# Second mixer's small products as column halves: state outputs, chunk scores, and the order of the states

## The chip, the cores and the metric

The kernel runs on one core of one Trainium2 chip. The metric is the device time of one execution in microseconds; the times below are medians of several runs. The engines are called as in the profile: PE is TensorE (PEld its weight loads), DVE is VectorE, ACT is ScalarE, POOL is GpSimd, SP is the queue that issues most of the DMAs.

## The reference

A two-layer decoder trunk on one sequence of 256 tokens, width 1024, in float32. Layer 0 uses a windowed attention mixer, layer 1 a gated linear attention (GLA) in chunks of 64 tokens with 4 heads (keys of 128, values of 256); each mixer is followed by a gated feed-forward part of width 2816 with a short convolution. The change lies in the GLA mixer:

```python
q_t = q * jnp.exp(bcum)
k_t = k * jnp.exp(-bcum)
k_d = k * jnp.exp(blast - bcum)
A = jnp.where(causal, jnp.einsum('bhncd,bhnsd->bhncs', q_t, k_t), 0.0)   # scores of a chunk, 64 x 64
o_intra = jnp.einsum('bhncs,bhnse->bhnce', A, v)
kv = jnp.einsum('bhncd,bhnce->bhnde', k_d, v)                           # what a chunk adds to the state
...
state = dec[..., None] * state + inc                                    # scan over the 4 chunks
o = o_intra + jnp.einsum('bhncd,bhnde->bhnce', q_t, s_prev)             # the state's share of the output
```

Behind it follow a norm over each head, a gate `silu(r)` and the output projection.

## The kernel before

Activations stand transposed in SBUF: partitions are features, columns the 256 tokens. Large products are split into high and low float32r parts, three matmuls for one (`mm3`, lines 216 to 218); a weight tile of 128x2048 is loaded by SP (`split`, line 185), its high part made by ACT (line 191) and its low part by DVE (line 195), out of rings of four raw and three split buffers. The small products of the GLA mixer are plain float32; each of them is two LDWEIGHTS and two MATMUL instructions in the profile.

The GLA mixer treats its four heads in two pairs. For each pair:

- `masked` (lines 1113 to 1131) transposes `k_d` (line 1121, bank `kdt`) and makes the scores (line 1124, bank `a`). Two chunks are done at once: a tile of 128 tokens holds two chunks, the product is 128x128, and only its two diagonal blocks of 64x64 are wanted. ACT copies the transposed keys (line 1128), and DVE copies the scores under the mask `causal` (line 1130, COPY_PREDICATED) into `a_t`, which POOL has set to zero.
- `states` (lines 1133 to 1154) makes what chunks 0, 1 and 2 add to the state (line 1140). Chunk n lies in partitions 0 to 63 (n even) or 64 to 127 (n odd) of its tile, so the contraction uses one half of the rows of the array. ACT copies the first state (line 1146), DVE does the scan (line 1152).
- `outputs` (lines 1156 to 1181) makes the output: first scores by values (line 1164), then, accumulated in the same bank, state by queries for chunks 1 to 3 (line 1170): 128 stationary columns, 64 moving columns, 12 products for a pair of heads.
- `normed_outputs` sums squares (line 1194 on PE, from `osq`, line 1190 on DVE) and scales.

The order on PE is fixed by hand here: `in_turn` puts each group of products behind the one before. Between the groups stand the halves of the gate's large product (`gate`, bank `pr`) and of the last heads' queries and keys (`keyed`, bank `pqk`). The order is: scores of heads 0 and 1 within `keyed(2)`, their states, scores of heads 2 and 3 within `gate(0)`, outputs of heads 0 and 1, states of heads 2 and 3, and within `gate(1)` the norm of the first pair and the outputs of the second. `behind(i)` only orders an instruction after another for the planner; within one group, and for the other engines, the planner (the tile framework, which lays instructions out by a modelled timeline) chooses the order. Within the first call of `masked` it places the scores of the first head ahead of the transposes of the second.

In the first mixer, `outputs` (lines 577 and 581, bank `po`) has products with 64 stationary columns, whose results go by turns to partitions 0 to 63 and 64 to 127; `scores` (line 524, bank `s`) has 64 by 64 blocks.

Of the kernel before, what the change touches and what calls it, by code (L numbers as in the profile page):

```python
# [14 lines left out]
U32 = mybir.dt.uint32  # L15
# [3 lines left out]
P = 128  # L19
D = 1024  # L20
T = 256
# [7 lines left out]
CH = 64  # L29
# [28 lines left out]
def trunk(ctx: ExitStack, tc: tile.TileContext, I, out):  # L58
    nc = tc.nc
# [16 lines left out]
    mm = nc.tensor.matmul  # L76
# [28 lines left out]
    ident = const.tile([P, P], F32, name="ident")  # L105
# [13 lines left out]
    @contextmanager  # L119
    def behind(*those):  # L120

        with ExitStack() as st:
            for i in those:
                st.enter_context(tc.issue_after(i.ins))
            yield

    def keep_warm(n, ps=None):

        ps = bank("warm", "p") if ps is None else ps
        for i in range(n):  # L130
            i = mm(ps[:, :P], ones_d, ones_d, start=True, stop=True)
        return i
# [80 lines left out]
    def mm3(ps, a, b, start, stop):  # L213


        mm(ps, a[0], b[0], start=start, stop=False)  # L216
        mm(ps, a[0], b[1], start=False, stop=False)  # L217
        return mm(ps, a[1], b[0], start=False, stop=stop)  # L218
# [6 lines left out]
    def rstd_of(squares, n=D, tag=None, between=None):  # L225
        ps = bank("ms", tag)
        a = None
        for i, sq in enumerate(squares):
            if i and between:
                with behind(a):  # L230
                    a = between()
            with behind(*((a,) if between and a else ())):
                a = mm(ps[:, :T], ones_d, sq, start=(i == 0), stop=(i == len(squares) - 1))
        ln = tmp.tile([P, T], F32, tag="ln", name="ln", bufs=2)
        nc.scalar.activation(ln, ps[:, :T], AF.Ln, bias=eps[:, 0:1], scale=D / n)
        r = tmp.tile([P, T], F32, tag="rstd", name="rstd", bufs=2)
        norm_ops[:] = a, nc.scalar.activation(r, ln, AF.Exp, scale=-0.5)
        return r
# [117 lines left out]
    def parts(w, at, n=P):  # L356
        return w[0][:, at : at + n], w[1][:, at : at + n]
# [43 lines left out]
    r = rstd_of([sq[:, 0, :], sq[:, 4, :]], tag="p", between=lambda: keep_warm(1, warm_ps))  # L401
# [107 lines left out]
    def scores(q, k):  # L509


        s = [bank("s", "s") for _ in range(4)]
        for h in range(2):
            n = T + 2 * h
            for i, (a, b) in enumerate(((0, 0), (1, 0), (0, 1))):
                for hh, e in enumerate(heads):
                    last = mm(s[2 * h + hh][:, 0:n], q[0][a][e, P * h : P * h + P], k[0][b][e, 0:n], start=(i == 0), stop=(i == 2))
        own_keys = [(h, g, hh, odd) for h in range(2) for g in (1, 2) for hh, odd in ((0, 0), (1, 1), (0, 1), (1, 0))]
        with behind(last):
            for h, g, hh, odd in own_keys:  # L520
                at = T + 2 * h + CH * (g - 1)
                e, to = heads[hh], slice(CH * odd, CH * odd + CH)
                own = slice(P * h + CH * odd, P * h + CH * odd + CH)
                last = mm(s[2 * h + hh][to, at : at + CH], q[g][e, own], k[g][e, own], start=True, stop=True)
        return s, last
# [38 lines left out]
    def turn(tiles, normed_p, pt):  # L564
        for i in tiles:
            t = bank("t", "ttss"[i])
            for j in range(3):
                c = slice(P * j, P * j + P)
                last = nc.tensor.transpose(t[:, c], normed_p[i][:, c], ident)  # L569
            pt_copy[0] = nc.scalar.copy(pt[:, i, :], t[:, 0:KEYS])  # L570
        return last
# [105 lines left out]
    last = [warm]  # L677
# [43 lines left out]
    with behind(end):  # L721
        s, last = scores(*qk0)
# [12 lines left out]
    with behind(end):  # L735
        s, last = scores(*qk1)
    raised = maxima(s, bias1)

    for u in range(2, NPAIR):
# [11 lines left out]
        with behind(end):  # L751
            turned = turn((2, 3), *before)
# [10 lines left out]
        if u == 2:  # L763
            with behind(end):
                turned = turn((2, 3), *before)
        if u < NPAIR - 1:
            end = values(u, 1, pv)
        with behind(end, turned):
            s, last = scores(*qk)
        with behind(last):  # L770
            last = outputs(u - 1, v, before[1])
# [171 lines left out]
    def gt(shape, name, dt=F32, bufs=1, tag=None):  # L943
        return gla.tile(shape, dt, tag=tag or name, name=name, bufs=bufs)
# [16 lines left out]
    causal = gt([P, 2, P], "causal")  # L961
# [74 lines left out]
    for n in range(4):  # L1036
# [7 lines left out]
        for i in range(2):  # L1044
            kt = 2 * n + i
            for t in range(2):
                ht = [y[:, P * t : P * t + P] for y in h[kt]]
                for s in range(2):
                    with behind(*last_gate if kt == 5 else ()):
                        last = mm3(pv[t][s], ht, parts(w, D * i + 512 * s, 512), kt == 0, kt == KT - 1)  # L1050
# [57 lines left out]

    last_st, kv_copy = [None], [None]

    def masked(tag, *two):
        turned, pa = bank("kdt", tag), bank("a", tag)
        kd = gt([P, 2 * T], "kdT", bufs=2)
        a_t = [gt([P, 2, P], "a_t", bufs=4) for _ in two]
        halves = [(i, t, slice(T * i + P * t, T * i + P * t + P)) for i in range(2) for t in range(2)]
        for to in a_t:
            nc.gpsimd.memset(to, 0.0)

        def products():
            for i, t, c in halves:  # L1120
                nc.tensor.transpose(turned[:, c], two[i][2][:, P * t : P * t + P], ident)
            for i, t, c in halves:
                own = slice(P * t, P * t + P)
                last = mm(pa[:, c], two[i][1][:, own], two[i][0][:, own], start=True, stop=True)
            return last

        in_turn(products)
        nc.scalar.copy(kd, turned)
        for i in range(2):
            nc.vector.copy_predicated(a_t[i], causal.bitcast(U32), pa[:, T * i : T * i + T].rearrange("p (a b) -> p a b", a=2))  # L1130
        return kd, a_t

    def states(first, kd):
        kv = [bank("kv", tag) for tag in ("s", "s", "t" if first else "s")]

        def products():
            for i in range(2):
                for n in range(3):
                    t, r = n // 2, slice(CH * (n % 2), CH * (n % 2) + CH)
                    last = mm(kv[n][:, T * i : T * i + T], kd[r, T * i + P * t : T * i + P * t + P],  # L1140
                              v[t][r, T * (first + i) : T * (first + i) + T], start=True, stop=True)
            return last

        in_turn(products)
        st = [gt([P, 2 * T], f"st{n}") for n in range(3)]
        kv_copy[0] = nc.scalar.copy(st[0], kv[0])
        for n in (1, 2):
            for i in range(2):
                part = min(first + i, 1)
                at = 4 * (first + i - PARTS[part][0]) + n  # L1150
                c = slice(T * i, T * i + T)
                last_st[0] = nc.vector.scalar_tensor_tensor(st[n][:, c], st[n - 1][:, c], gates[part][3][:, at : at + 1], kv[n][:, c],
                                                            op0=ALU.mult, op1=ALU.add)
        return st

    def outputs(first, two, a_t, st):
        po = [bank("o", "s") for _ in range(2)]

        def products():
            for i in range(2):  # L1160
                for et in range(2):
                    ev = slice(T * (first + i) + P * et, T * (first + i) + P * et + P)
                    for t in range(2):
                        mm(po[i][:, T * et + P * t : T * et + P * t + P], v[t][:, ev], a_t[i][:, t, :],
                           start=(et == t == 0), stop=False)
            for i in range(2):
                for et in range(2):
                    for n in range(1, 4):
                        c = slice(CH * n, CH * n + CH)
                        last = mm(po[i][:, T * et + CH * n : T * et + CH * n + CH],  # L1170
                                  st[n - 1][:, T * i + P * et : T * i + P * et + P], two[i][0][:, c],
                                  start=False, stop=(et == 1 and n == 3))
            return last

        in_turn(products)
        sq = gt([P, 4 * T], "osq", tag="D1").rearrange("p (i e t) -> p i e t", i=2, e=2)
        for i in range(2):
            nc.scalar.activation(sq[:, i, :, :], po[i].rearrange("p (e t) -> p e t", e=2), AF.Square)
        acc = gt([P, 2 * T], "oacc", tag="keys", bufs=2).rearrange("p (i t) -> p i t", i=2)
        nc.vector.tensor_tensor(acc, sq[:, :, 0, :], sq[:, :, 1, :], op=ALU.add)  # L1180
        return po, acc
# [99 lines left out]
    two = [decayed(0, *keyed(0, w[0]))]  # L1281
# [72 lines left out]
    with behind(last_pd[0]):  # L1354
        last = mean_square([0])
    with behind(last):
        last = turned(range(2))
    with behind(last):
        last = mean_square([1])
# [4 lines left out]
    r = tmp.tile([P, 4], F32, tag="m", name="rstd")  # L1364
    nc.scalar.activation(r, ln, AF.Exp, scale=-0.5)
    y = wspl.tile([P, 2048], F32, tag="whi", name="y")
    for half in range(2):
        for t, own in enumerate(halves):
            c = slice(512 * half, 512 * half + 512)
# [118 lines left out]
```

## Time and profile before

| | us |
|---|---|
| median of 3 runs | 756.48 (756.15 to 757.1) |
| the profiled execution | 758.08 |
| its span, first to last instruction | 756.0 |
| mean granted TensorE clock | 0.998 |
| second mixer's small products on PE | about 495.9 to 529.3 us of the span |

A row of the groups gives line, engine, operation, output and inputs, tile, shapes, count, then the busy time in us, the mean of one in ns, and the idle time before it with what ended it. A row of the waits gives who waited for whom: us in total, times, longest. A row of the timeline gives start (us from the span's start), length, engine, line, operation and count; rows of one group are merged. `128*64` is the part of the array in use, rows by stationary columns; `128x64` after it is the moving operand. Matmuls overlap in the array, so their lengths add up to more than their time.

### The profile page before, as it was taken

The numbers are of one execution on the slowest core, as the hardware profiler recorded it, in microseconds if no ns is written. First come the engines' busy times: TensorE is split into PE (matmuls) and PEld (weight loads), VectorE is DVE, ScalarE is ACT, GpSimd is POOL, SyncE is SP. The second block draws the span as 40 slices with busy tenths as digits, with TensorE's granted clock in tenths as the row PEclk, the third lists the DMA queues.
The fourth block names the chain that finished last, engine by engine and source line by source line (L and its number), as shares of the span: only waits on it lengthen the run. The fifth ranks groups of instructions, "written<-read, shape, count | busy, mean of one in ns | idle before, by whom it ended". The sixth has DMA issues, their size and how long they took to land.

```text
span 756.0 us, 15974 instructions
## 1 busy us (share of the span) xinstructions
PE 747.9 (99%) x6410; PEld 727.1 (96%) x6410; DVE 629.3 (83%) x1120; ACT 489.9 (65%) x954; POOL 77.6 (10%) x148
## 2 busy tenths in 40 slices
PE   9999999999999999999999999999999999999997
PEld 7999999999999999999999998999999999999997
DVE  7989977887888688999988778986897989898662
ACT  6467677566575588776766456844878766666552
POOL 6342320220200010000000002000010000000100
PEclk9999999999999999999999999999999999999999
DMA  9999789888886566766656985864475755556651
GB/s 341 417 348 370 252 291 311 293 269 292 286 279 235 215 223 230 278 231 235 219 183 223 340 293 191 332 248 137 144 279 175 272 194 197 207 173 215 222 188 56
DMA packets 31996, 186.83 MB, mean 247 GB/s; under 512 B 4385, under 2 KB 4769, under 8 KB 16050
## 3 DMA queue, kind: packets, MB, share of 16 engines
q1 hardware_dynamic: 26816, 162.38, 60.4%
q0 software_dynamic: 4784, 23.09, 9.6%
q8 instruction: 50, 0.82, 0.4%
q10 hardware_dynamic: 322, 0.35, 0.1%
q14 instruction: 24, 0.20, 0.1%
HBM read 184.70 MB, written 1.10 MB: 246 GB/s over the span
## 4 chain that ended last, share of the span: by engine, by line
PE 86%; DVE 7%; DMA 4%; ACT 2%; issue 1%; ACTq 0%; DVEq 0%
PE pab L216 10%; PE pab L217 10%; PE pab L218 10%; PE pqk L216 5%; PE pd L218 4%; PE pqk L217 4%; PE pqk L218 4%; PE pd L217 4%; PE pd L216 4%; PE pv L217 3%; PE pv L218 3%; PE pv L216 3%; PE py L217 2%; PE py L216 2%; PE py L218 2%; PE t L569 1%
## 5 line engine op out<-in xcount | busy, mean ns | idle before, releaser
L195 DVE TENSOR_TENSOR wlo<-raw,whi 128x1024 fp32r<-128x1024 f32 (+3 forms) x254 | 272.0, 1103 | 53.7 <-ACT whi L191 52.7
L191 ACT CAST whi<-raw 128x1024 fp32r<-128x1024 f32 (+3 forms) x254 | 228.2, 947 | 104.5 <-PE pab L217 41.4
L218 PE MATMUL pab<-hhi,wlo 128*128 128x256 f32 x672 | 184.9, 276 | 0.0
L217 PE MATMUL pab<-hlo,whi 128*128 128x256 f32 x672 | 184.8, 277 | 0.0
L216 PE MATMUL pab<-hhi,whi 128*128 128x256 f32 x672 | 183.4, 277 | 0.0
L218 PEld LDWEIGHTS pab<-hhi,wlo 128*128 128x128 f32 x672 | 126.2, 188 | 0.0
L217 PEld LDWEIGHTS pab<-hlo,whi 128*128 128x128 f32 x672 | 126.0, 188 | 0.2
L216 PEld LDWEIGHTS pab<-hhi,whi 128*128 128x128 f32 x672 | 125.2, 188 | 0.1
L218 PE MATMUL pd<-ghi,wlo 128*128 128x256 f32 x352 | 97.3, 277 | 0.3 <-DVE wlo L195 0.2
L217 PE MATMUL pd<-glo,whi 128*128 128x256 f32 x352 | 97.1, 276 | 0.0
L216 PE MATMUL pd<-ghi,whi 128*128 128x256 f32 x352 | 96.8, 276 | 0.0
L216 PE MATMUL pqk<-hhi,whi 128*128 128x256 f32 x314 | 88.2, 281 | 0.0
L217 PE MATMUL pqk<-hlo,whi 128*128 128x256 f32 x314 | 87.0, 277 | 0.0
L218 PE MATMUL pqk<-hhi,wlo 128*128 128x256 f32 x314 | 87.0, 277 | 0.0
L161 DVE CUSTOM_DVE_ANT_0 ada_raw<-ada_raw,c_bc 128x1024 f32<-128x1024 f32 x52 | 61.4, 1220 | 11.9 <-DMA ada_raw<-in_w_ada 11.8
L218 PEld LDWEIGHTS pd<-ghi,wlo 128*128 128x128 f32 x352 | 66.1, 188 | 0.7 <-DVE wlo L195 0.7
L217 PEld LDWEIGHTS pd<-glo,whi 128*128 128x128 f32 x352 | 66.1, 188 | 0.0
L216 PEld LDWEIGHTS pd<-ghi,whi 128*128 128x128 f32 x352 | 65.9, 188 | 0.0
L216 PEld LDWEIGHTS pqk<-hhi,whi 128*128 128x128 f32 x314 | 59.1, 188 | 0.4
L217 PEld LDWEIGHTS pqk<-hlo,whi 128*128 128x128 f32 x314 | 59.0, 188 | 0.0
L218 PEld LDWEIGHTS pqk<-hhi,wlo 128*128 128x128 f32 x314 | 59.0, 188 | 0.0
L897 ACT ACTIVATE r<-pab,small 128x256 f32<-128x256 f32 x86 | 46.7, 559 | 15.5 <-DVE r L900 15.5
(244 smaller groups left out, 1504.1 us busy)
## 6 DMA issues: line engine op xcount, KB each, us to landing
raw<-in_w_up SPq DMA_DIRECT2D x42, 1024.0 KB, 4.9
ada_raw<-in_w_ada SPq DMA_DIRECT2D x24, 1024.0 KB, 5.2
raw<-in_w_down SPq DMA_DIRECT2D x32, 704.0 KB, 5.6
raw<-in_wqk SPq DMA_DIRECT2D x18, 1024.0 KB, 7.5
raw<-in_wv SPq DMA_DIRECT2D x14, 768.0 KB, 6.3
early_x<-in_w_ada POOLq DMA_DIRECT2D x9, 1024.0 KB, 7.8
x_all<-in_w_ada POOLq DMA_DIRECT2D x9, 1024.0 KB, 6.0
raw<-in_w_out_a SPq DMA_DIRECT2D x4, 1024.0 KB, 6.8
```

Of the source, the lines that this page charges most:

```text
L161: last_dot[0] = nc.vector.tensor_tensor_reduce(w, w, c_bc, op0=ALU.mult, op1=ALU.add, scale=1.0, scalar=0.0, accum_out=dot,)
L191: copied[0] = nc.scalar.copy(hi[:, c], raw[:, c])
L195: last_lo[0] = nc.vector.tensor_tensor(lo[:, c], raw[:, c], hi[:, c].bitcast(F32), op=ALU.subtract)
L216: mm(ps, a[0], b[0], start=start, stop=False)
L217: mm(ps, a[0], b[1], start=False, stop=False)
L218: return mm(ps, a[1], b[0], start=False, stop=stop)
L569: last = nc.tensor.transpose(t[:, c], normed_p[i][:, c], ident)
L897: nc.scalar.activation(r, u[:, :T], AF.Identity, scale=cw[2], bias=col(C_CB + 44 * l + f))
```

## The change

- The state outputs (line 1170) are issued as two products each, one for each half of the stationary columns; the halves write partitions 0 to 63 and 64 to 127 of the bank.
- The chunk scores (line 1124) are issued as the two 64x64 blocks of the diagonal instead of a product of 128x128, each behind the instruction before it, and all behind the transposes.
- The masked copy (line 1130) is done for each block alone: two instructions of 64 partitions for each head.
- The states (line 1140) are issued in an order in which chunks 0 and 1 of both heads come first and chunk 2 of both heads last. Their number and shapes stay.

```diff
+    sides = [slice(CH * odd, CH * odd + CH) for odd in range(2)]
+
     def masked(tag, *two):
...
             for i, t, c in halves:
-                nc.tensor.transpose(turned[:, c], two[i][2][:, P * t : P * t + P], ident)
+                last = nc.tensor.transpose(turned[:, c], two[i][2][:, P * t : P * t + P], ident)
             for i, t, c in halves:
-                own = slice(P * t, P * t + P)
-                last = mm(pa[:, c], two[i][1][:, own], two[i][0][:, own], start=True, stop=True)
+                for to in sides:
+                    own, at = (slice(z + to.start, z + to.stop) for z in (P * t, c.start))
+                    with behind(last):
+                        last = mm(pa[to, at], two[i][1][:, own], two[i][0][:, own], start=True, stop=True)
             return last
...
         for i in range(2):
-            nc.vector.copy_predicated(a_t[i], causal.bitcast(U32), pa[:, T * i : T * i + T].rearrange("p (a b) -> p a b", a=2))
+            for to in sides:
+                from_pa = pa[to, T * i : T * i + T].rearrange("p (a b) -> p a b", a=2)[:, :, to]
+                nc.vector.copy_predicated(a_t[i][to, :, to], causal[to, :, to].bitcast(U32), from_pa)
         return kd, a_t
...
         def products():
-            for i in range(2):
-                for n in range(3):
-                    t, r = n // 2, slice(CH * (n % 2), CH * (n % 2) + CH)
-                    last = mm(kv[n][:, T * i : T * i + T], kd[r, T * i + P * t : T * i + P * t + P],
+            for i, n in ((0, 0), (0, 1), (1, 0), (1, 1), (0, 2), (1, 2)):
+                t, r = n // 2, slice(CH * (n % 2), CH * (n % 2) + CH)
+                last = mm(kv[n][:, T * i : T * i + T], kd[r, T * i + P * t : T * i + P * t + P],
                               v[t][r, T * (first + i) : T * (first + i) + T], start=True, stop=True)
             return last
...
                     for n in range(1, 4):
                         c = slice(CH * n, CH * n + CH)
-                        last = mm(po[i][:, T * et + CH * n : T * et + CH * n + CH],
-                                  st[n - 1][:, T * i + P * et : T * i + P * et + P], two[i][0][:, c],
-                                  start=False, stop=(et == 1 and n == 3))
+                        for to in sides:
+                            at = T * i + P * et + to.start
+                            last = mm(po[i][to, T * et + CH * n : T * et + CH * n + CH], st[n - 1][:, at : at + CH], two[i][0][:, c],
+                                      start=False, stop=(et == 1 and n == 3))
             return last
```

## The prediction

> **What bounds the kernel now.** I read the page first (busy time by engine, the chain that ended last), then TensorE's own waits over the second layer, then the groups of instructions of the second mixer, and last the timeline of the places where these groups stand.
>
> ```profile
> span 756.0 us, 15974 instructions
> PE 747.9 (99%) x6410; PEld 727.1 (96%) x6410; DVE 629.3 (83%) x1120; ACT 489.9 (65%) x954; POOL 77.6 (10%) x148
> PE 86%; DVE 7%; DMA 4%; ACT 2%; issue 1%; ACTq 0%; DVEq 0%
> ```
> ```profile
> PE pd L218 <- DVE wlo L195: 0.2, 1, 0.2
> PE ms L1351 <- ACT sq L245: 0.2, 1, 0.2
> PE a L1124 <- DVE q_t L1106: 0.2, 1, 0.2
> PE pv L217 <- DVE wlo L195: 0.2, 1, 0.2
> ```
>
> TensorE (PE) is busy 99% of the span and 86% of the chain that ended last. The second fence is the whole of TensorE's waits from 450 us to the end: four of 0.2 us. So from the second mixer on nothing but TensorE's own stream sets the time, and a microsecond taken out of that stream is a microsecond off the end, as long as no new wait opens.
>
> The change touches three TensorE groups and one of DVE; the largest and the last:
>
> ```profile
> L1170 PE MATMUL o<-q_t,st 128*128 128x64 f32 x48 | 5.6, 273 | 0.0
> ```
> ```profile
> L1130 DVE COPY_PREDICATED a_t<-causal,a 128x256 f32<-128x256 uint32 x4 | 1.6, 444 | 0.7 <-PE a L1124 0.7
> ```
>
> Each float32 product is two instructions (24 state products, x48). A mean of 273 ns is latency; matmuls overlap, so the cost is the distance from one start to the next, read from the timeline (start, length, line, count):
>
> ```profile
> 496.69 0.38 PE L1121 MATMUL kdt<-ident,keys 128*128 128x128 f32 x2
> 497.26 0.71 PE L1124 MATMUL a<-q_t,keys 128*128 128x128 f32 x4 [0.19 <-DVE q_t L1106]
> ...
> 497.93 0.28 PE L217 MATMUL pqk<-lv,whi 128*128 128x256 f32 x1
> ```
> ```profile
> 511.46 1.06 PE L1124 MATMUL a<-q_t,keys 128*128 128x128 f32 x8
> 512.28 0.36 PE L216 MATMUL pr<-lv,whi 128*128 128x256 f32 x1
> 512.48 0.28 PE L217 MATMUL pr<-lv,whi 128*128 128x256 f32 x1
> ```
> ```profile
> 516.97 2.79 PE L1170 MATMUL o<-q_t,st 128*128 128x64 f32 x24
> 519.69 1.99 PE L1140 MATMUL kv<-v,kdT 64*128 64x256 f32 x12
> ```
> ```profile
> 526.73 2.79 PE L1170 MATMUL o<-q_t,st 128*128 128x64 f32 x24
> 529.33 0.36 PE L216 MATMUL pr<-lv,whi 128*128 128x256 f32 x1
> 529.53 0.28 PE L217 MATMUL pr<-lv,whi 128*128 128x256 f32 x1
> ```
>
> Chunk scores (moving width 128) stand 0.82/8, about 0.11 us, apart; state outputs (moving width 64) stand 2.72/24 = 0.113 us apart. Half the moving width saves nothing: what both share is a stationary operand of 128 columns. That is the time the change goes for.
>
> **The change, part by part.** The shape that it introduces, 128 rows by 64 columns with 64 moving, and the two column halves in turn, already runs in the first mixer:
>
> ```profile
> 257.69 0.28 PE L218 MATMUL py<-ohi,wlo 128*128 128x256 f32 x1
> 257.81 0.28 PE L216 MATMUL py<-ohi,whi 128*128 128x256 f32 x1
> 258.01 1.08 PE L577 MATMUL po<-pt,v 128*64 128x256 f32 x8
> 258.93 0.64 PE L581 MATMUL po<-pt,v 128*64 128x64 f32 x16
> 259.49 0.38 PE L217 MATMUL py<-olo,whi 128*128 128x256 f32 x1
> 259.71 0.29 PE L218 MATMUL py<-ohi,wlo 128*128 128x256 f32 x1
> ```
> ```profile
> 131.09 0.39 PE L577 MATMUL po<-pt,v 128*64 128x256 f32 x2
> 131.30 0.63 PE L581 MATMUL po<-pt,v 128*64 128x64 f32 x16
> ```
> ```profile
> L581 PE MATMUL po<-pt,v x128: 219/222/222, 88.8 to 259.3; 128*64 128x64 f32 x128
> ```
>
> Line 581: 0.63 us from the first start to the last end, less the 0.22 of one, is 0.41 us over seven steps, if two instructions (one per half) start together: 0.058 us a pair, 0.029 us an instruction. Going in and out of this shape costs extra. In: 257.81 to 258.01 is 0.20 where the matmul before it took 0.12 (0.08 over), and the eight of line 577 take 0.92 where four pairs at 0.21 (131.09 to 131.30) would take 0.84 (0.08 over): 0.16. Out: 258.93 to 259.49 is 0.56 for eight pairs worth 0.47 (0.09 over), then 259.49 to 259.71 is 0.22 (0.10 over): 0.19.
>
> *State outputs, first call.* Now 516.97 to 519.69, 2.72 us. After: in 0.16, then 48 instructions as 24 pairs x 0.058 = 1.39, then into line 1140, which splits the array by rows. No row shows that step. Its bounds are nothing and the full 0.19 of a step out; I take 0.11, near the 0.09 that the first half of a step out costs, since line 1140 pays for its own start already now: 1.66. Gain 1.06 (0.98 to 1.17).
>
> *State outputs, second call.* Now 526.73 to 529.53, up to the second matmul of the gate, 2.80 us. After: 0.16 + 1.39 + 0.19 + the 0.12 of the first gate matmul = 1.86. Gain 0.94.
>
> *Chunk scores, second call.* Now 511.46 to 512.48, 1.02 us. After: 16 instructions, 8 pairs x 0.058 = 0.46, and 0.16 + 0.19 + 0.12: 0.93. Gain 0.09; the two switches eat most of it.
>
> *Chunk scores, first call.* Now two heads are interleaved, and the last four instructions wait for `q_t` at 497.26. The new chain puts all four transposes first; the third needs `keys` of the second head, there by the 496.69 row, so TensorE idles while it now does the first head's scores. From about 496.9 it has room for the switch in (0.16) and four pairs of the first head (0.23), and at 497.26 it still waits for `q_t`. After that: four pairs 0.23, a refill of 0.10 (the row's 0.71 against 3 x 0.11 + 0.27 for four that need not wait), out 0.19 and 0.12: 0.64 against the present 0.67. Gain 0.03; from 0 to 0.2.
>
> *States in a new order.* Of twelve instructions, eight use partitions 0 to 63 in either order and four use 64 to 127. Eight at the 0.21 of line 577's pairs are 1.68 us, and the row has 1.99 from the first start to the last end, with the switch in and the tail of the last one: the four others already run beside the eight. Gain 0 (at best the 0.31 between, at worst one lost overlap, 0.21, in each call). Its one effect is that the first state bank is complete about two steps of 0.21 us earlier, for ACT, which is not late.
>
> *Masked copies.* Four copies of 256 elements (444 ns) become eight of 128. No row has that copy; between half the present one (222 ns) and all of it, the nearest row is a 128-wide DVE pass at 284 ns, which I take:
>
> ```profile
> L558 DVE TENSOR_SCALAR pn<-prob,m 128x128 f32<-128x128 f32 x32 | 9.1, 284 | 0.0
> ```
> ```profile
> 500.84 0.42 DVE L1104 TENSOR_TENSOR keys<-pqk,e_d 128x256 f32<-128x256 f32 x1 [0.68 <-PE pqk L218]
> ```
>
> That is 4 x 284 - 2 x 444 ns = 0.25 us more DVE time in each call. In the first it lies under DVE's 0.68 us idle before the next `keys`; at the full price, 0.89, these would be 0.2 us late, and only the chunk scores at 511.46 use them. Cost 0.
>
> *Sum.* 1.06 + 0.94 + 0.09 + 0.03 = 2.12 us off TensorE's stream. Cover: TensorE gets ahead of DVE by up to 0.94 us between the two output calls. What is nearest to late is the norm of the second pair:
>
> ```profile
> 531.81 0.69 DVE L1190 TENSOR_TENSOR osq<-oacc,osq 128x512 fp32r<-128x512 f32 x1 [0.69 <-ACT osq L1189]
> ```
> ```profile
> 534.93 0.62 PE L1194 MATMUL ms<-osq,ones_r 128*128 128x512 f32 x2
> ```
>
> Its input is ready at 532.50, 2.4 us ahead; 1.5 would remain. Later, in the last feed-forward part, ACT's weight copies wait for TensorE to free their buffers, so that DMA, ACT and DVE move with it:
>
> ```profile
> ACT whi L191 <- PE pab L217: 41.4, 27, 2.4
> ```
>
> The profiled execution took 758.08 us (span 756.0) against a median of 756.48: 756.0 by its own time, a span of 753.9, and **754.4 for the median**.
>
> **The rivals.** *Halves that run one at a time (slower).* The new code issues 128 narrow instructions where 64 wide ones stood; eight fall into the wait for `q_t`, 120 count. Line 581 shows 0.029 us each in runs of 16, never of 48. If a long run falls to one at a time, 0.058 each, 120 x 0.029 = 3.48 us are added to the forecast: 757.9. It decides from 0.029 + 2.12/120 = 0.047 us each. Against it: the densest stretch shown,
>
> ```profile
> 100.12 0.69 PE L524 MATMUL s<-k,q 64*64 64x64 f32 x32
> 100.74 1.08 PE L577 MATMUL po<-pt,v 128*64 128x256 f32 x8
> 101.66 0.63 PE L581 MATMUL po<-pt,v 128*64 128x64 f32 x16
> 102.26 0.38 PE L216 MATMUL pqk<-hhi,whi 128*128 128x256 f32 x1
> ```
>
> is 56 in 2.14 us from 100.12 to 102.26, 0.038 each with its switches. The Trainium skill, page "TensorE: Matmul & The Clock Gate", section "Wait — 56ns, not 53.3ns?", gives a case that speaks for this rival: with hardware decode off the sequencer spends about 62 ns per matmul, which binds when the array needs less; by that figure, an estimate, the kernel would end near 758.4. The 0.038 us stand against it, though a filled queue could hide it over a stretch this short.
>
> *The gain is given back (no change).* For: TensorE's waits are nil because the planner has put DVE and ACT work where it fits, and it plans anew from the modelled length of the changed products. A weight split is two of these:
>
> ```profile
> L195 DVE TENSOR_TENSOR wlo<-raw,whi 128x1024 fp32r<-128x1024 f32 (+3 forms) x254 | 272.0, 1103 | 53.7 <-ACT whi L191 52.7
> ```
>
> One, 2.2 us, ahead of `q_t` or of line 1190 costs 2.2 us less the slack: at `q_t`, where slack is nil, all of it, 756.6; at 1190, 0.7, 755.1. Against: most of the order here is fixed by hand.
>
> *More than forecast.* If the switches hide behind the filling pipeline, the narrow runs alone count: 2 x (2.70 - 1.39) + 0.43 + 0.2 = 3.2, 753.3. The Trainium skill's "TensorEngine Tiling (Array Packing)", section "Theoretical Speedup", has up to 2x for a dimension of 64; the rows show that (0.113 to 0.058), but only between switches.
>
> **How the numbers follow.** Forecast 754.4 (its own range 753.9 to 754.9): 0.56. Given back in part or whole, 755.0 to 756.7: 0.22. One at a time, 757.9 and above: 0.10, half of it beyond 758.0. A new order that costs more than it saves, above 758.0: 0.07. More, 753.3: 0.05. Faster or slower counts beyond 0.2%, 1.5 us, about what a measurement of this kernel tells from none: faster is the forecast and "more" less a little at 755.0, 0.59; slower 0.12; the same 0.29. The range 753.5 to 757.0 leaves out "more" and most of the two slow cases.
>
> **What would show it.** Line 1170's successor: x48 a call in about 1.6 us, pairs 0.058 apart; scores x16 in the second call in 0.6; line 1140 still 1.99; eight masked copies near 280 ns; span 753.9; no TensorE wait over 0.3 us after 500. I am wrong if the spacing is over 0.047, if a switch costs over 0.5, or if a new wait of TensorE on DVE stands in the list.

## The result and the profile after

The kernel after takes 754.76 us (median of 8 runs, 753.59 to 755.71) against 757.61 for the kernel before beside it (756.15 to 758.37, 8 runs): a ratio of 0.9965 [0.9955, 0.9974]. A second comparison, with other runs, gave 0.9974 [0.9963, 0.9985] (below). The forecast was 754.4 against 756.48, a ratio of 0.9972. The profiled execution took 754.74 us, with a span of 753.0 where 753.9 was forecast.

The page of after, its span, busy time and the engines' shares of the chain that ended last:

```profile
span 753.0 us, 16106 instructions
PE 745.0 (99%) x6474; PEld 723.7 (96%) x6474; DVE 630.5 (84%) x1124; ACT 491.5 (65%) x954; POOL 78.2 (10%) x148
...
PE 88%; DVE 5%; DMA 3%; ACT 2%; issue 1%; SPq 0%; ACTq 0%; DVEq 0%
```

TensorE is still the only bound: it has 64 more instructions (6410 to 6474) and 2.9 us less busy time. Its waits from 450 us to the end:

```profile
PE kdt L1123 <- DVE keys L1104: 0.2, 1, 0.2
PE ms L1357 <- ACT sq L245: 0.2, 1, 0.2
PE pv L217 <- DVE wlo L195: 0.2, 1, 0.2
```

The wait for `q_t` has become one for the second head's `keys`, of the same length. No new wait opened. The timeline of TensorE at the four places that the prediction costed (start, length, line, count; transposes are now line 1123, scores 1128, states 1145, scores by values 1169, state outputs 1177):

```profile
496.04 0.38 PE L1123 MATMUL kdt<-ident,keys 128*128 128x128 f32 x2
496.62 0.44 PE L1123 MATMUL kdt<-ident,keys 128*128 128x128 f32 x2 [0.20 <-DVE keys L1104]
496.99 0.75 PE L1128 MATMUL a<-q_t,keys 128*64 128x64 f32 x16
...
497.88 0.28 PE L217 MATMUL pqk<-lv,whi 128*128 128x256 f32 x1
...
511.51 0.69 PE L1128 MATMUL a<-q_t,keys 128*64 128x64 f32 x16
...
512.35 0.28 PE L217 MATMUL pr<-lv,whi 128*128 128x256 f32 x1
...
516.93 1.62 PE L1177 MATMUL o<-q_t,st 128*64 128x64 f32 x48
518.48 1.99 PE L1145 MATMUL kv<-v,kdT 64*128 64x256 f32 x12
...
525.61 1.62 PE L1177 MATMUL o<-q_t,st 128*64 128x64 f32 x48
527.16 0.38 PE L216 MATMUL pr<-lv,whi 128*128 128x256 f32 x1
527.38 0.28 PE L217 MATMUL pr<-lv,whi 128*128 128x256 f32 x1
```

Read against the same rows of before (the mixer starts within 0.01 us of the same place in both), the lead grows like this:

| place | before | after | lead | new lead | forecast |
|---|---|---|---|---|---|
| behind the first scores (L217) | 497.93 | 497.88 | 0.05 | 0.05 | 0.03 |
| behind the second scores (L217) | 512.48 | 512.35 | 0.13 | 0.08 | 0.09 |
| behind the first state outputs (`kv`) | 519.69 | 518.48 | 1.21 | 1.08 | 1.06 |
| behind the second (L217 of the gate) | 529.53 | 527.38 | 2.15 | 0.94 | 0.94 |

The sum is 2.15 us; 2.12 was forecast. Behind the gate the lead neither grows nor shrinks for 170 us: the same product of line 218 near 700 us, of before and then of after, stands 2.14 apart.

```profile
700.05 0.28 PE L218 MATMUL pd<-ghi,wlo 128*128 128x256 f32 x1
```
```profile
697.91 0.28 PE L218 MATMUL pd<-ghi,wlo 128*128 128x256 f32 x1
```

The span shrank by 3.0. The other 0.85 us does not belong to the change; experiment 4 deals with it.

### The profile page after: what moved, and what is told of

It reads as the page before. It is cut to its first block, busy times and chain, and to the rows that moved or that the text cites. A ratio compares the mean times of both kernels' runs of the same rounds, so it can differ in the third digit from the quotient of the medians.

```text
span 753.0 us, 16106 instructions
## 1 busy us (share of the span) xinstructions
PE 745.0 (99%) x6474; PEld 723.7 (96%) x6474; DVE 630.5 (84%) x1124; ACT 491.5 (65%) x954; POOL 78.2 (10%) x148
## 4 chain that ended last, share of the span: by engine, by line
PE 88%; DVE 5%; DMA 3%; ACT 2%; issue 1%; SPq 0%; ACTq 0%; DVEq 0%
PE pab L216 10%; PE pab L217 10%; PE pab L218 10%; PE pd L216 5%; PE pd L217 5%; PE pd L218 5%; PE pqk L216 5%; PE pqk L217 4%; PE pqk L218 4%; PE pv L217 3%; PE pv L218 3%; PE pv L216 3%; DMA early_x<-in_w_ada 2%; PE py L217 2%; PE py L218 2%; PE py L216 2%
## 5 line engine op out<-in xcount | busy, mean ns | idle before, releaser
L217 PE MATMUL pab<-hlo,whi 128*128 128x256 f32 x672 | 184.8, 277 | 0.0
L217 PEld LDWEIGHTS pab<-hlo,whi 128*128 128x128 f32 x672 | 126.0, 188 | 0.2
L217 PE MATMUL pd<-glo,whi 128*128 128x256 f32 x352 | 97.1, 276 | 0.0
L217 PE MATMUL pqk<-hlo,whi 128*128 128x256 f32 x314 | 87.0, 277 | 0.0
L217 PEld LDWEIGHTS pd<-glo,whi 128*128 128x128 f32 x352 | 66.1, 188 | 0.0
L217 PEld LDWEIGHTS pqk<-hlo,whi 128*128 128x128 f32 x314 | 59.0, 188 | 0.0
```

## The experiments

**1. State outputs alone.** Of the change only the part in `outputs`:

```diff
+                        for to in sides:
+                            at = T * i + P * et + to.start
+                            last = mm(po[i][to, ...], st[n - 1][:, at : at + CH], two[i][0][:, c], ...)
...
```

> State outputs as column halves alone; scores, masked copies and order of the states as before. Theory (column pairs, 0.029 us an instruction, about 0.35 us for a switch in and out): each call of the state outputs takes 1.55 to 1.65 us instead of 2.72, TensorE is 2.0 to 2.1 us ahead of the profile before at 530 us, time 2.0 to 2.8 us below the kernel before, depending on the two waits of the last feed-forward part. Rival (half of the gain is due to the scores or to the states' order): less than 1.5 us ahead at 530 us.

Measured: 754.65 us (754.23 to 755.33) against 756.53 (756.18 to 757.38), 0.9974 [0.9964, 0.9984]. Its timeline on TensorE:

```profile
516.40 1.62 PE L1174 MATMUL o<-q_t,st 128*64 128x64 f32 x48
517.94 1.99 PE L1142 MATMUL kv<-v,kdT 64*128 64x256 f32 x12
```

The 1.54 us to the states are those of after. This part alone gives what the timing can tell of the change. TensorE's lead over the first profile of before grows by 1.8 us between 492 and 530 us of before's span, where 2.0 to 2.1 was expected: the two calls bring 1.06 and 0.93, and 0.2 is lost between 504 and 512 us, ahead of both, in products of line 216 to 218 that stand about 0.117 us apart in this execution and 0.113 in that of before (the last section returns to these two steps).

**2. Chunk scores alone** (with the masked copies):

```diff
+                for to in sides:
+                    own, at = (slice(z + to.start, z + to.stop) for z in (P * t, c.start))
+                    with behind(last):
+                        last = mm(pa[to, at], two[i][1][:, own], two[i][0][:, own], start=True, stop=True)
...
```

> Chunk scores as 64 by 64 blocks of the diagonal and masked copies by blocks alone; state outputs and order of the states as before. Theory (two switches eat nearly all of it): first call 0 to 0.1 us, second call about 0.1 us less, TensorE 0.1 to 0.2 us ahead at 530 us; no change of the time that can be measured. Rival (scores carry a third of the gain): 0.7 us ahead.

Measured: 756.68 us, 1.0002 [0.9993, 1.0011], beside the same runs of before. The first call in its timeline:

```profile
495.39 0.38 PE L1123 MATMUL kdt<-ident,keys 128*128 128x128 f32 x2
...
496.31 0.75 PE L1128 MATMUL a<-q_t,keys 128*64 128x64 f32 x16
...
497.21 0.28 PE L217 MATMUL pqk<-lv,whi 128*128 128x256 f32 x1
```

From the first transposes to line 217 it is 1.82 us, where before has 1.90 (its transposes start at 496.03): 0.08 gained. The second call brings another 0.08, and at 530 us the lead over before has grown by 0.23 in all, a little over the 0.1 to 0.2 that was expected; the rival's 0.7 is out. That is too little for the timing to tell, as the sizes 0.03 and 0.09 had said.

**3. Order of the states alone:**

```diff
-            for i in range(2):
-                for n in range(3):
+            for i, n in ((0, 0), (0, 1), (1, 0), (1, 1), (0, 2), (1, 2)):
```

> Only the order of the states is changed. Theory (four of the six products use the lower half of the rows in either order, so it makes no difference on TensorE): line of the states takes 1.92 us in both calls as before, 0 ahead at 530 us, no change of the time. Rival (neighbours of the same half were a stall): 0.2 us less in each call, 0.4 ahead.

Measured: 756.71 us, 1.0 [0.9991, 1.001]. Its timeline has the two calls at the length of before:

```profile
500.24 1.99 PE L1139 MATMUL kv<-v,kdT 64*128 64x256 f32 x12
...
519.20 1.99 PE L1139 MATMUL kv<-v,kdT 64*128 64x256 f32 x12
```

No change to the hundredth, in either place. (The 1.92 us of the expectation are the distance to the next product; the row's 1.99 runs to the end of its last instruction.)

**4. The kernel before, once more** (no edit), because its first profile had more to lose than the change could give:

> The kernel before, unchanged, for a second profile of it and for the noise of the comparison. The profile before had two waits of TensorE near 708 and 725 us for a weight split behind a slow adaLN load (7.5 us to landing); the profile after had neither, and gained 0.8 us there. Theory (the slow loads were chance in that one execution): here the loads land in about 5 us, the waits are absent or of another size, span 755.0 to 756.0. Rival (the schedule before always has them): both waits again, 0.4 and 0.3 us, span 755.8 to 756.2.

Measured: 756.99 us, 1.0001 [0.9991, 1.001]; span 755.1, 0.9 less than in the first profile. The first profile has two gaps on TensorE in the last feed-forward part, which the second has not:

```profile
707.65 0.28 PE L217 MATMUL pd<-glo,whi 128*128 128x256 f32 x1
708.15 0.38 PE L218 MATMUL pd<-ghi,wlo 128*128 128x256 f32 x1 [0.23 <-DVE wlo L195]
708.37 0.29 PE L216 MATMUL pd<-ghi,whi 128*128 128x256 f32 x1
...
725.16 0.28 PE L217 MATMUL pd<-glo,whi 128*128 128x256 f32 x1
725.48 0.38 PE L218 MATMUL pd<-ghi,wlo 128*128 128x256 f32 x1
725.71 0.28 PE L216 MATMUL pd<-ghi,whi 128*128 128x256 f32 x1
```

From 707.65 to 708.37 is 0.72 us where two steps of 0.113 are 0.23, and from 725.16 to 725.71 is 0.55: together 0.8 lost. The list of waits, from which the prediction worked, shows 0.2 of the first and nothing of the second, because the recorded ends of the matmuls cover part of each gap; the distance between starts shows all of it. The DMA view of that stretch (690 to 756 us) in the same profile, with the time from issue to landing as its last column:

```profile
ada_raw<-in_w_ada SPq DMA_DIRECT2D x2, 1024.0 KB, 7.5
```

DVE waits in order for these two, and the weight split queued behind them is late. In the second profile they land in 5.8 us, in that of after in 5.2. DVE's idle time for this tile on the pages of the first profile of before, of after, and of this second profile of before, in that order:

```profile
L161 DVE CUSTOM_DVE_ANT_0 ada_raw<-ada_raw,c_bc 128x1024 f32<-128x1024 f32 x52 | 61.4, 1220 | 11.9 <-DMA ada_raw<-in_w_ada 11.8
```
```profile
L161 DVE CUSTOM_DVE_ANT_0 ada_raw<-ada_raw,c_bc 128x1024 f32<-128x1024 f32 x52 | 61.4, 1222 | 8.2 <-DMA ada_raw<-in_w_ada 8.2
```
```profile
L161 DVE CUSTOM_DVE_ANT_0 ada_raw<-ada_raw,c_bc 128x1024 f32<-128x1024 f32 x52 | 61.4, 1221 | 8.1 <-DMA ada_raw<-in_w_ada 8.1
```

The unchanged kernel has the wait in one execution and not in another, so the 0.8 us is no part of the change. Counted at the same products, every later profile but that of experiment 6, changed kernel or not, gains the same 0.85 us on the first profile of before between 700 and 730 us. (On the way there the second profile is 0.5 ahead by 115 us and gives that back between 572 and 582 us; the last section says how.) Why the two loads took 7.5 us that time is not settled.

**5. One column half after the other.** The kernel after, with the state outputs issued as all products of half 0 and then all of half 1:

```diff
-            for i in range(2):
-                for et in range(2):
-                    for n in range(1, 4):
-                        for to in sides:
+            for to in sides:
+                for i in range(2):
+                    for et in range(2):
+                        for n in range(1, 4):
...
+                            with behind(*run_out):
...
```

> The changed kernel, but the state outputs of a call run all products of column half 0 first and then all of half 1, instead of the two halves by turns. Theory (the gain is two column halves of the array at work at once, each with its own stream of 0.058 us an instruction, and only neighbouring instructions of different halves can overlap): 48 x 0.058 = 2.8 us a call, as the kernel before, span 753.0 + 2 x 1.2 = about 755.4. Rival A (each instruction costs 0.029 us by itself because its stationary operand is half as wide, whatever runs beside it): the row of 48 stays near 1.6 us a call, span near 753. Rival B (the halves overlap over a long look-ahead in the queue): 1.4 to 1.6 us too, but then the records of half 1 start together with those of half 0, far ahead of their place in the program.

Measured in one execution: 758.24 us, span 756.1, before 757.14 (756.78 to 758.52) in the same session. Its timeline:

```profile
517.58 2.83 PE L1179 MATMUL o<-q_t,st 128*64 128x64 f32 x48
520.34 1.99 PE L1145 MATMUL kv<-v,kdT 64*128 64x256 f32 x12
...
527.47 2.83 PE L1179 MATMUL o<-q_t,st 128*64 128x64 f32 x48
530.24 0.38 PE L216 MATMUL pr<-lv,whi 128*128 128x256 f32 x1
```

The same 48 instructions now need 2.76 and 2.77 us, as the wide ones did. In the single records (one instruction each, where the rows above merge them) the instructions of one half stand 0.058 us apart, half the 0.113 of a wide one; but there are two of them for each wide one, so by itself the narrower shape gains nothing. The gain is that two halves run at once. Rival A (0.029 us an instruction whatever runs beside it) falls. Two calls cost 2 x 1.21 = 2.4 us against after; the span is 3.1 longer, and the rest, 0.7, stands in the trace already at 64 us, ahead of anything that was edited. Rival B (a long look-ahead) falls as well: in the single records the first instruction of half 1 starts 0.17 us ahead of the last of half 0, with three instructions of half 0 still to come. TensorE reaches some three instructions ahead here, no more.

**6. One half left out.** The kernel after, without 10 of the 12 pairs of instructions of half 1 in each call:

```diff
-                        for to in sides:
+                        for to in sides if et == 1 and n == 3 else sides[:1]:
```

> The changed kernel with most of the second column half of the state outputs left out (of the 24 narrow products of a call, the 12 of half 0 and the last of half 1 for each head remain: 28 instructions in place of 48; the other half's share of the state outputs is missing). Theory (two streams at once, 0.058 us an instruction in each): half 0 alone still takes 24 x 0.058 = 1.39 us plus its tail, so the row stays near 1.6 us a call and the time near that of the changed kernel, 0 to 0.3 us less. Rival (0.029 us an instruction in single file): 28 x 0.029 = 0.81 us, the row near 1.0 us a call, 1.2 us less over both calls.

Its timeline:

```profile
515.80 1.61 PE L1177 MATMUL o<-q_t,st 128*64 128x64 f32 x28
517.35 1.99 PE L1145 MATMUL kv<-v,kdT 64*128 64x256 f32 x12
```

24 of the 28 lie in half 0. The 28 take the 1.55 us of 48. The half that was left out had cost nothing, which says the same from the other side.

The whole kernel did not stay near after, though: 755.9 us (755.44 to 757.64), 0.9983 [0.9974, 0.9992], 0.5 above the kernel after in the same session. TensorE and DVE near the norm of the second pair, in this kernel:

```profile
532.02 0.50 PE L1200 MATMUL ms<-osq,ones_r 128*128 128x512 f32 x1 [0.22 <-ACT osq L1195]
533.07 0.50 PE L1200 MATMUL ms<-osq,ones_r 128*128 128x512 f32 x1 [0.54 <-DVE osq L1196]
```
```profile
530.05 2.36 DVE L195 TENSOR_TENSOR wlo<-raw,whi 128x1024 fp32r<-128x1024 f32 x2 [1.31 <-ACT whi L191]
532.33 0.68 DVE L1196 TENSOR_TENSOR osq<-oacc,osq 128x512 fp32r<-128x512 f32 x1
```

And in the kernel after:

```profile
530.56 0.69 DVE L1196 TENSOR_TENSOR osq<-oacc,osq 128x512 fp32r<-128x512 f32 x1 [0.69 <-ACT osq L1195]
531.51 2.36 DVE L195 TENSOR_TENSOR wlo<-raw,whi 128x1024 fp32r<-128x1024 f32 x2 [0.26 <-ACT whi L191]
```

With 40 instructions fewer in its model the planner put the weight split (ACT's copy and DVE's low part) ahead of the norm's squares, and TensorE waits 0.22 + 0.54 us. This is the prediction's rival "the gain is given back", at the place and price that it named (line 1190 of before, 0.7 us). It did not come about in the change itself.

**7. Four quarters.** The kernel after, with state outputs in four quarters of 32 columns by turns, 96 instructions a call:

```diff
-                        for to in sides:
-                            at = T * i + P * et + to.start
+                        for z in range(0, P, 32):
+                            at = T * i + P * et + z
...
```

> The changed kernel, but the state outputs in four column quarters of 32 columns by turns (96 instructions a call). Theory (each column group streams its 64 moving columns in 0.058 us, groups beside each other): 24 groups of four x 0.058 = 1.39 us, the row near 1.6 us a call as with halves, no further gain; span near 753. Rival (the time of an instruction falls with its columns, 0.015 us each): also 1.4, so this run does not tell that one. Rival (TensorE cannot issue faster than one instruction in 0.029 us): 96 x 0.029 = 2.8 us a call, and the gain of the outputs, some 2 us, is gone, span near 755. Rival (a floor of 62 ns an instruction, an estimate from the Trainium skill's page TensorE: Matmul & The Clock Gate): 96 x 0.062 = 6 us a call, span near 762.

Measured in one execution: 755.26 us, span 753.3. Its timeline:

```profile
516.59 1.55 PE L1177 MATMUL o<-q_t,st 128*32 128x64 f32 x96
518.07 1.99 PE L1145 MATMUL kv<-v,kdT 64*128 64x256 f32 x12
```

1.48 us for 96 instructions, 0.0154 us each. Twice the instructions cost nothing, so TensorE's issue is no bound here; what is left is the 24 instructions in each column group, 0.056 us apart in the single records. So the step of one stream fell from 0.113 to 0.058 us when its stationary columns went from 128 to 64, and hardly at all when they went to 32: with 64 moving columns a narrower stationary operand brings no more. With that the last ground for the rival "halves that run one at a time" is gone. The Trainium skill, page "TensorE: Matmul & The Clock Gate", section "Wait — 56ns, not 53.3ns?", names 62 ns per matmul for a sequencer without hardware decode; a run of 96 at 15 ns shows no such bound in this kernel. The 0.07 us a call that quarters save is below what timing can tell, so no better version follows from this.

**8. The kernel after, once more** (no edit):

> The changed kernel again, beside the others. Inside the second mixer the same distances as in its first profile (outputs 1.62, scores 0.69, states 1.99 us a call). Theory (the change is worth 2.1 to 2.2 us on TensorE, and the rest of the first difference, some 0.5 us, was the weight loads of one execution of the kernel before): the ratio to the kernel before is 0.9965 to 0.9980, a little nearer to 1 than in the first comparison, 754.4 to 755.0 us at a kernel before of 756.5. Rival (the change also frees weight loads late in the kernel, worth 0.5 to 0.8 us more): 0.9960 to 0.9965 again.

Measured: 755.42 us (754.58 to 756.27) against 757.14, 0.9974 [0.9963, 0.9985]; span 753.6. The state outputs:

```profile
517.10 1.62 PE L1177 MATMUL o<-q_t,st 128*64 128x64 f32 x48
518.65 1.99 PE L1145 MATMUL kv<-v,kdT 64*128 64x256 f32 x12
```

1.55 us again. The ratio is on the side of the theory (0.9965 to 0.9980), with an interval that does not exclude the rival.

## Why the prediction was right, step by step

- *TensorE alone sets the time.* Held: 2.15 us out of its stream, no new wait over 0.2 us behind it, and the lead still 2.14 at 700 us.
- *0.058 us a pair, also in runs of 48.* Held. The records stand 0.058 us apart in each half, and the second half's start 0.007 us behind the first's. Experiments 5 to 7 show why: the halves are two streams side by side, each with the step that it has alone, and issue does not bind them.
- *The switches.* In: 0.16 forecast. In the single records the last instruction of line 1169 and the first of line 1177 stand 0.205 us apart, where before has 0.111 in that place, 0.09 over; and the second instruction of a half stands 0.107 behind the first, 0.05 over: 0.14. Out to the states: the last instruction of a half starts 23 steps and 0.05 after the first, 1.39, and one more step makes 1.45; 1.55 leaves 0.10, against the 0.11 that was taken between bounds of 0 and 0.19 without a row for it. Out to the gate: 0.10 + 0.10 = 0.20 against 0.19.
- *Scores.* The mechanism of the first call was right (all transposes first, TensorE idle at the second head's `keys`, its scores held by `q_t` all the same: they start 0.05 us behind the end of `q_t`, at 497.28, as in before), its size 0.05 against 0.03. In the second the two switches eat most of the gain, 0.08 against 0.09.
- *States in a new order: 0.* Held: 1.99 us in every run. In the single records of before, eight starts of a call stand in a row, 0.216 us apart behind the first, and the other four beside them, which fits the eight instructions of partitions 0 to 63 and the four of 64 to 127; by this reading the third of the four, ninth in the program, starts at 501.27, ahead of three that stand earlier in it. The overlap that an order could bring was there.
- *Masked copies at 284 ns, hidden.* The group of after:

```profile
L1136 DVE COPY_PREDICATED a_t<-causal,a 64x128 f32<-64x128 uint32 x8 | 2.4, 302 | 0.6 <-PE a L1128 0.5
```

302 ns against an estimate of 284; 2.4 us in place of 1.6, and hidden, since no wait names it.
- *Cover at the norm.* 1.5 us was to remain. The squares of after end at 531.25 (the DVE row above), and TensorE takes them here:

```profile
532.78 0.62 PE L1200 MATMUL ms<-osq,ones_r 128*128 128x512 f32 x2
```

1.5 us remain. Experiment 6 shows how a change of plan uses them up.
- *Where it was off.* The span: 753.0 and 753.6 in two executions against 753.9. The reference point was an execution with 0.8 us of gaps that the kernel does not always have, and that the list of waits did not show in full. From the second profile of before, 755.1 - 2.15 = 753.0; that this agrees to a tenth is chance, since executions of one kernel differ by more (spans of 751.8 to 753.6 for the kernel after). The median: 754.76 against 754.4, closer than the difference behind it. The kernel before came out at 757.61 beside it, not at the 756.48 that the forecast started from, and the medians differ by 2.85 us in that comparison and by 1.72 in the second. The medians alone leave the gain between these two; it is the timeline that confirms the 2.12.

## What to carry to other kernels

Here a product had a moving operand narrower than its stationary one (64 columns against 128). Splitting the stationary columns in halves **issued by turns** took 12 such products (24 wide instructions) from 2.72 to 1.55 us; the turns are what does it, since the same halves one after the other gain nothing. That the moving operand should be the narrower one is read from the steps and not from a run: with 128 stationary columns 64 and 128 moving ones both stand about 0.11 us apart, while with 64 stationary columns it is 0.058 us for 64 moving ones and 0.21 for 256 (line 577). Charge some 0.14 us in and 0.1 to 0.2 us out for each run of such products, so that 12 products are worth it (0.94 to 1.08 us) and the four chunk scores hardly are (0.08). With TensorE at 99% the gain reaches the end only as long as the planner leaves the order of ACT and DVE alone: compare that order before believing a gain or a loss.

## What the runs showed that was not expected

The wide products (moving 256) have two steps, at a granted clock of 1.00. This is TensorE's last feed-forward part, 709 to 744 us, in the profile of experiment 6 and then of after; the number in brackets behind PE busy counts its instructions:

```profile
709.00:744.00 35.00, 35.00 (x299) 35.00 (x299) 20.38 (x31) 15.66 (x27) 1.19 (x1) 1.00 0.52 177
```
```profile
709.00:744.00 35.00, 35.00 (x311) 35.00 (x310) 19.03 (x29) 15.12 (x26) 1.19 (x1) 1.00 0.39 136
```

299 against 311 in 35 us: 0.117 us apart against 0.113, with one gap of 0.07 us in the first and none in the second. In experiment 6 the slower step sets in right behind one wait:

```profile
706.12 0.28 PE L217 MATMUL pd<-glo,whi 128*128 128x256 f32 x1
706.71 0.38 PE L218 MATMUL pd<-ghi,wlo 128*128 128x256 f32 x1 [0.32 <-DVE wlo L195]
706.93 0.28 PE L216 MATMUL pd<-ghi,whi 128*128 128x256 f32 x1
707.05 0.28 PE L217 MATMUL pd<-glo,whi 128*128 128x256 f32 x1
```

It then lasts to the end of the part, 1.4 us over 35, and that execution is the slowest of its kernel (757.64 against a median of 755.9). The first profile of before has such a wait at 708.15 and keeps the faster step. Other stretches change in the same way between executions, near 100 to 113 and 572 to 582 us for two, each worth 0.4; and some stand at the slower step in both kernels, such as the 21 steps from 512.59 to 515.07 us in the profile of before (0.118 each). What decides was not found; for this kernel it means that two profiles of one program can differ by a microsecond with no wait to show for it.
